# A second ending by tokens for the last half of a hybrid encoder layer, and large tiles at multiples of 512 bytes

## The chip, the cores and the metric

One core of a Trainium2 chip. The metric is the device time of one execution in microseconds (us), the median of three runs.

## The reference

One encoder layer over 512 tokens with 1024 features, in float32:

```
x = x + 1/2 * swiglu(rmsnorm(x), gate1, up1, down1)       # 1024 -> 2816 -> 1024
h = rmsnorm(x); P = h @ w_in                              # 1024 -> 3072
y = concat(rmsnorm(hyena(P[:, :1536])), rmsnorm(attention(P[:, 1536:])))
x = x + y @ w_out
x = x + 1/2 * swiglu(rmsnorm(x), gate2, up2, down2)
out = rmsnorm(x)            # x * rsqrt(mean(x*x) + 1e-6) * gain, per token
swiglu(h, g, u, d) = (silu(h @ g) * (h @ u)) @ d
```

Hyena is two long convolutions with gates, done through Fourier tables; the attention is a mixture of dilated windows. Neither is touched by the change.

## The kernel before

**Layout.** Features stand on partitions: `x` is eight tiles of 128 features x 512 tokens. Every large product is split in three (`mm3`, lines 144 to 148): each operand is a rounded high part and a low part, and high x high, high x low and low x high are added up in one PSUM bank. In a call the first operand is the one loaded into the array (a weight load, `PEld` in the profile), the second is streamed. In the FFNs and the projections weights are loaded and 512 tokens are streamed. Weights come in chunks of 128 x 1024, which ScalarE rounds (`wh`) and VectorE subtracts (`wl`).

**The FFN** (`ffn`, from line 319) runs twice over halves of the 22 hidden blocks: 11 times a gate and an up product of eight blocks each (`pgu`, streaming `xh`/`xl`), then the down product of the half, eight output blocks of 11 (`pd`, streaming `gh`/`gl`, the rounded and the low part of the hidden values). In the last half of the second FFN the output blocks 6 and 7 are done for one half of the tokens and then for the other: four groups of 33 matmuls with 256 columns. `tail` (line 1231) ends each: it adds the result to `x`, squares it, and sums over features with matmuls against `ones`. After block 7 it takes root and reciprocal, spreads the reciprocal over partitions with two matmuls against the identity (`spread`, line 312, tile `pb`), multiplies all eight blocks of `x` with it and sends them in four transfers of 256 KB, by turns on ScalarE's and SyncE's queue.

`done2` (line 1225) runs for blocks 0 to 5 when they are complete: their squares are added into `ssq` on GpSimd, and ScalarE multiplies them by the final gain.

**The order** of instructions on each engine is fixed while the program is built by a planner (`Merge`, line 71): streams of work ask for an engine with an estimated cost, and the one that can start first goes first, with a priority on ties.

**Where tiles stand.** A pool's tiles lie one behind the other in the order in which they are first asked for, each rounded up to 32 bytes. The main pool (`g.wp`, line 1110) starts at 16,512 bytes: `x` 16 KB, `cols` 352 bytes, `eps`, `ones` 512 bytes, `warm`, then raw and split weights, the identity, `xh`, `xl`, `ssq` and so on, and four small tiles for root and reciprocal at its end. The stages' pools stand behind it, those of side "right" at the upper end. So the large tiles start at these distances behind a multiple of 512: `x` 128, `ones` 0, all weight chunks, the identity, `xh`, `xl`, `ssq` 32, all of the stages' left pools (`z`, `u`, `gh`, `gl`, `yg`) 160, and the filter stage's tables and tiles (`ftab`, `fh`, `fl`) 480.

Of the kernel before, what the change touches and what calls it, by code (L numbers as in the profile page):

```python
# [35 lines left out]
NG1, NGM, NGH, NGA, NG2, NGF, NCW, NCB = 0, 8, 16, 20, 24, 32, 40, 76  # L36
NCOL = 88
WR, WB, HQ, SB, UC, ZB, X1B, UR = 2, 3, 3, 3, 3, 3, 3, 3
TWO_PI = 2.0 * math.pi


# [25 lines left out]
def wait(ev):  # L67
    return "W", ev
# [172 lines left out]
class SumSq:  # L241
# [38 lines left out]
    def rstd_cols(self, n, lag, res, m, ev):  # L280


        g, nc = self.g, self.g.nc
        yield on_v(0.0, lag)
        parts = self.sums()
        yield on_p(0.9 * len(parts), ps=1)
        pc = psum(g, "pc")
        for b in range(4):
            for i, t in enumerate(parts):
                nc.tensor.matmul(pc[:, b:b + 1], t[:, b * P:(b + 1) * P], g.ones[:, 0:1],  # L290
                                 start=i == 0, stop=i == len(parts) - 1)
        yield on_v(0.5, 0.4)
        std = g.wp.tile([P, 4], F32, tag="std", name="std", bufs=2)
        nc.scalar.activation(std, pc[:, 0:4], AF.Sqrt, bias=g.eps, scale=1.0 / n)
        rc = g.wp.tile([P, 4], F32, tag="rc", name="rc", bufs=2)
# [23 lines left out]
def ffn(g, m, fp, xg, nrm, nev, done, tail=None):  # L319
# [31 lines left out]
    for h in range(2):  # L351
        for f in range(HALF):
            pgu = []
            for _ in range(2):
                wc = g.w.take()
                ps = psum(g, "pgu")
                for k in range(DT):
                    if k == 3:
                        m.spawn(g.w.tick(), -1)
                    if k % 2 == 0:  # L360
                        yield on_p(1.3, 0.0, ps=int(k == 0))
                    mm3(nc, ps, wblk(wc, k), xg[k], k == 0, k == DT - 1)
                pgu.append(ps)
            ev = evs[h, f] = Event()
            m.spawn(evac(f, *pgu, ev), 0)
        wc, used = None, 8
        nd = DT - 2 if h == 1 and tail else DT
        for d in range(nd):
            ps = psum(g, "pd")
            for k in range(HALF):  # L370
                if used == 8:
                    wc, used = g.w.take(), 0
                if used == 3:
                    m.spawn(g.w.tick(), -1)
                if d == 0:
                    yield wait(evs[h, k])
                yield on_p(0.65, 0.0, ps=int(k == 0))
                mm3(nc, ps, wblk(wc, used), gt[k], k == 0, k == HALF - 1)
                used += 1
            m.spawn(devac(d, ps, h == 1), 0)  # L380
        if nd == DT:
            continue
        blk = []
        for th in range(2):
            for d in range(nd, DT):
                ps = psum(g, "pd")
                for k in range(HALF):
                    if th == 0:
                        if used == 8:
                            wc, used = g.w.take(), 0  # L390
                        if used == 3:
                            m.spawn(g.w.tick(), -1)
                        blk.append(wblk(wc, used))
                        used += 1
                    yield on_p(0.32, 0.0, ps=int(k == 0))
# [38 lines left out]
def filters(g, m, pool, tpool, a, start, done):  # L434
# [668 lines left out]
def body(ctx: ExitStack, tc: tile.TileContext, a: dict, out: bass.AP):  # L1103
# [19 lines left out]
    g.warm = warm = g.wp.tile([P, 1], F32, tag="warm", name="warm")  # L1123
    nc.scalar.activation(warm, g.eps, AF.Silu)
    ps = psum(g, "warm")
    for _ in range(NWARM):
# [5 lines left out]
        if d == 1:  # L1132
            g.w.start()
    g.w.load(1)
    g.ident = g.wp.tile([P, P], F32, tag="ident", name="ident")
    make_identity(nc, g.ident)


# [78 lines left out]

    with pool("f2", **over) as fp:
        ss3 = SumSq(g)
        n2, nev = {}, Event()  # L1220
        gain = lambda d: g.cols[:, NGF + d:NGF + d + 1]
        sq = {}
# [8 lines left out]
        def tail(d, th, ps):  # L1231

            hs = slice(th * CW, (th + 1) * CW)
            x = g.x[d][:, hs]
            if d == DT - 2:
                yield on_p(0.4, 0.0, ps=1)
                pc.append(psum(g, "pc"))
                for b in range(2):
                    bs = slice((2 * th + b) * P, (2 * th + b + 1) * P)
                    nc.tensor.matmul(pc[th][:, b:b + 1], ss3.acc[:, bs], g.ones[:, 0:1],  # L1240
                                     start=b == 0, stop=False)
            yield on_v(0.35)
            nc.vector.scalar_tensor_tensor(out=x, in0=ps[:, 0:CW], scalar=0.5, in1=x,
# [4 lines left out]
            nc.scalar.activation(sq[d][:, 0:CW], x, AF.Square)  # L1248
            yield on_p(0.3)
            for b in range(2):  # L1250
                nc.tensor.matmul(pc[th][:, b:b + 1], sq[d][:, b * P:(b + 1) * P],
                                 g.ones[:, 0:1], start=False, stop=d == DT - 1 and b == 1)
            if d < DT - 1:
                return
            yield on_v(0.3, 0.6)
            std = g.wp.tile([P, 4], F32, tag="std", name="std", bufs=2)
            nc.scalar.activation(std[:, 0:2], pc[th][:, 0:2], AF.Sqrt, bias=g.eps, scale=1.0 / D)
            rc = g.wp.tile([P, 4], F32, tag="rc", name="rc", bufs=2)
            nc.vector.reciprocal(rc[:, 0:2], std[:, 0:2])
            yield on_p(0.5, 0.2, ps=1)  # L1260
            pb = psum(g, "pb")
            for b in range(2):
                spread(g, pb[:, b * P:(b + 1) * P], rc[:, b:b + 1], P)
            for c in range(DT // 2):
                yield on_v(0.7)
                o = g.wp.tile([P, 2, CW], F32, tag="xh", name="o", bufs=DT)
                for i in range(2):
                    e = 2 * c + i
                    if e < DT - 2:
                        nc.vector.tensor_tensor(out=o[:, i], in0=g.x[e][:, hs], in1=pb[:, 0:CW], op=ALU.mult)  # L1270
                    else:
                        nc.vector.scalar_tensor_tensor(out=o[:, i], in0=g.x[e][:, hs], scalar=gain(e),
                                                       in1=pb[:, 0:CW], op0=ALU.mult, op1=ALU.mult)
                (nc.sync if c % 2 else nc.scalar).dma_start(
                    out[2 * c:2 * c + 2, :, hs].rearrange("d p s -> p d s"), o)
            m.free(ps=2)

        m.spawn(ffn(g, m, fp, at.x2, n2, nev, done2, tail), 1)

# [2 lines left out]
            yield from ss2.rstd(D, L2, n2, m, nev)  # L1282

        m.spawn(norm2(), 0)
        m.run()


# [58 lines left out]
def _layout(i):  # L1346
# [7 lines left out]
        k, m = w.shape  # L1354
        return w.reshape(k // P, P, m // P, P).transpose(2, 1, 0, 3)

    def down(w):
        b = w.reshape(2, HALF, P, DT, P).transpose(0, 3, 1, 2, 4)
        b = b.reshape(2 * DT * HALF // 8, 8, P, P)
        return b.transpose(0, 2, 1, 3).reshape(-1, P, 1024)  # L1360

    for f in ("1", "2"):
        o[f"w{f}g"] = stationary(n[f"ffn{f}_w_gate"]).reshape(FT, P, 1024)
        o[f"w{f}u"] = stationary(n[f"ffn{f}_w_up"]).reshape(FT, P, 1024)
        o[f"w{f}d"] = down(n[f"ffn{f}_w_down"])
# [11 lines left out]
    o["fw1"] = n["hy_filt_w1"]  # L1377
    o["fw23"] = np.concatenate([n["hy_filt_w2"], n["hy_filt_w3"], n["hy_filt_w3"]], axis=1)
    o["fwo"] = n["hy_filt_w_out"].reshape(FW, 2, 2, C).transpose(1, 2, 0, 3).reshape(2, P, C)
    o["skip"] = n["hy_filt_skip"].reshape(1, 2 * C)  # L1380
    return {k: np.ascontiguousarray(v) for k, v in o.items()}

# [17 lines left out]
```

## Time and profile before

| | us |
|---|---|
| median of 3 runs | 1048.6 (1047.63 to 1049.46) |
| the profiled execution | 1048.07 |
| its span, first to last instruction | 1046.3 |
| TensorE busy | 1032.0 (99%) |
| VectorE busy | 604.5 (58%) |
| ScalarE busy | 402.5 (38%) |
| mean granted TensorE clock | 0.995 of 2.4 GHz |

PE is TensorE's matmuls, PEld its weight loads, DVE VectorE, ACT ScalarE, POOL GpSimd, SP SyncE. A matmul's own duration includes its way through the array and overlaps the next one; the pace is read from start to start. A line such as L146 is a line of the kernel; L146 to L148 are the three products of `mm3`. A matmul of plain float32 operands appears as two instructions.

### The profile page before, as it was taken

What the parts mean: (1) busy time and instruction counts of PE and PEld (TensorE: products, weight loads), DVE (VectorE), ACT (ScalarE), POOL (GpSimd) and SP (SyncE); (2) the same over time, 40 slices, a digit from 0 to 9 for tenths busy, and PEclk for the clock granted to TensorE, in tenths of its full rate; (3) what the DMA queues carried; (4) which work ended last, traced back from release to release, by engine and by line L of the source; (5) the groups of instructions that cost most, each with busy time, mean ns of one, the idle gap of its engine ahead of it and who ended that gap; (6) DMA issues with size and microseconds to landing.
All of it is one profiled execution on the core that took longest, in us unless ns stands there. A gap on an engine that the chain in (4) does not pass through costs nothing.

```text
span 1046.3 us, 12667 instructions
## 1 busy us (share of the span) xinstructions
PE 1032.0 (99%) x5012; PEld 844.7 (81%) x5012; DVE 604.5 (58%) x834; ACT 402.5 (38%) x594; POOL 45.9 (4%) x37
## 2 busy tenths in 40 slices
PE   9999999999999999999998999999999999999997
PEld 7877888888888888888886778888888888888886
DVE  5676646554676444887999744764453235444332
ACT  6433432233334332344347874543232213333341
POOL 4000000000000111000000000210000000000010
PEclk9999999999999999999999999999999999999998
DMA  6333423533255222234435311233322332332222
GB/s 216 129 124 106 126 91 118 174 98 104 91 170 171 92 90 91 66 114 143 143 105 186 122 42 61 81 101 101 101 89 93 101 100 86 96 101 101 93 69 81
DMA packets 43513, 114.25 MB, mean 109 GB/s; under 512 B 5082, under 2 KB 12314, under 8 KB 43453
## 3 DMA queue, kind: packets, MB, share of 16 engines
q1 hardware_dynamic: 41644, 111.30, 33.3%
q10 hardware_dynamic: 1808, 2.14, 0.6%
q8 instruction: 39, 0.64, 0.3%
q14 instruction: 22, 0.17, 0.1%
HBM read 106.08 MB, written 7.34 MB: 108 GB/s over the span
## 4 chain that ended last, share of the span: by engine, by line
PE 96%; DVE 2%; ACT 1%; issue 1%; DMA 1%; SPq 0%; DVEq 0%; ACTq 0%
PE pgu L146 15%; PE pgu L147 15%; PE pgu L148 15%; PE pd L146 8%; PE pd L148 8%; PE pd L147 8%; PE pp L146 3%; PE pp L148 3%; PE pp L147 3%; PE pw L146 2%; PE pw L148 1%; PE pw L147 1%; PE po L1008 1%; PE ppt L996 1%; PE pqk L1039 1%; PE pv L146 1%
## 5 line engine op out<-in xcount | busy, mean ns | idle before, releaser
L188 ACT ACTIVATE wh<-wr 128x1024 fp32r<-128x1024 f32 x159 | 168.5, 1060 | 411.9 <-PE pgu L147 143.1
L146 PE MATMUL pgu<-xh,wh 128*128 128x512 f32 x704 | 275.4, 391 | 0.4 <-ACT wh L580 0.4
L147 PE MATMUL pgu<-xl,wh 128*128 128x512 f32 x704 | 274.4, 390 | 0.3 <-DVE xl L236 0.3
L148 PE MATMUL pgu<-xh,wl 128*128 128x512 f32 x704 | 274.5, 390 | 0.1
L194 DVE TENSOR_TENSOR wl<-wr,wh 128x1024 fp32r<-128x1024 f32 x159 | 198.1, 1246 | 114.3 <-ACT wh L188 110.0
L146 PEld LDWEIGHTS pgu<-xh,wh 128*128 128x128 f32 x704 | 132.2, 188 | 31.0 <-issue 2.9
L147 PEld LDWEIGHTS pgu<-xl,wh 128*128 128x128 f32 x704 | 132.1, 188 | 29.6 <-DVE xl L236 1.4
L148 PEld LDWEIGHTS pgu<-xh,wl 128*128 128x128 f32 x704 | 132.1, 188 | 28.3 <-DVE wl L581 0.4
L146 PE MATMUL pd<-gh,wh 128*128 128x512 f32 (+1 forms) x374 | 143.2, 383 | 0.0
L147 PE MATMUL pd<-gl,wh 128*128 128x512 f32 (+1 forms) x374 | 142.7, 382 | 0.0
L148 PE MATMUL pd<-gh,wl 128*128 128x512 f32 (+1 forms) x374 | 142.7, 382 | 0.0
L256 POOL TENSOR_TENSOR ssq<-ssq,sq 128x512 f32<-128x512 f32 x31 | 45.2, 1457 | 975.5 <-ACT sq L252 974.6
L331 DVE TENSOR_TENSOR u<-pgu,rb 128x512 f32<-128x512 f32 x44 | 30.3, 690 | 97.3 <-PE pgu L148 97.3
L147 PEld LDWEIGHTS pd<-gl,wh 128*128 128x128 f32 x374 | 70.3, 188 | 15.1
L148 PEld LDWEIGHTS pd<-gh,wl 128*128 128x128 f32 x374 | 70.3, 188 | 15.0
L146 PEld LDWEIGHTS pd<-gh,wh 128*128 128x128 f32 x374 | 70.3, 188 | 15.0
L329 DVE TENSOR_TENSOR z<-pgu,rb 128x512 f32<-128x512 f32 x44 | 30.4, 691 | 60.6 <-PE pgu L148 60.5
L146 PE MATMUL pp<-xh,wh 128*128 128x512 f32 x128 | 50.0, 391 | 0.0
L147 PE MATMUL pp<-xl,wh 128*128 128x512 f32 x128 | 49.9, 390 | 0.0
L148 PE MATMUL pp<-xh,wl 128*128 128x512 f32 x128 | 49.8, 389 | 0.0
L343 DVE SCALAR_TENSOR_TENSOR x<-pd,x 128x512 f32<-128x512 f32 x30 | 20.7, 690 | 42.7 <-PE pd L148 42.6
L336 ACT ACTIVATE gh<-u 128x512 fp32r<-128x512 f32 x44 | 27.7, 632 | 24.2 <-DVE u L333 23.8
(207 smaller groups left out, 1189.3 us busy)
## 6 DMA issues: line engine op xcount, KB each, us to landing
wr<-w1u SPq DMA_DIRECT2D x22, 512.0 KB, 3.4
wr<-w1d SPq DMA_DIRECT2D x22, 512.0 KB, 3.4
wr<-w2g SPq DMA_DIRECT2D x22, 512.0 KB, 3.4
wr<-w2u SPq DMA_DIRECT2D x22, 512.0 KB, 3.4
wr<-w2d SPq DMA_DIRECT2D x22, 512.0 KB, 3.4
wr<-w1g SPq DMA_DIRECT2D x21, 512.0 KB, 3.4
wr<-win SPq DMA_DIRECT2D x16, 512.0 KB, 3.4
pe<-negb SPq DMA_DIRECT2D x32, 256.0 KB, 3.2
```

The lines of the kernel that those rows point to most:

```text
L146: nc.tensor.matmul(ps, lh, rh, start=start, stop=False)
L147: nc.tensor.matmul(ps, lh, rl, start=False, stop=False)
L148: nc.tensor.matmul(ps, ll, rh, start=False, stop=stop)
L188: self.g.nc.scalar.activation(self.hi[i], self.raw[i], AF.Copy)
L194: self.g.nc.vector.tensor_tensor(out=self.lo[i], in0=self.raw[i], in1=self.hi[i].bitcast(F32), op=ALU.subtract)
L256: g.nc.gpsimd.tensor_tensor(out=self.acc, in0=self.acc, in1=sq, op=ALU.add)
L329: nc.vector.tensor_tensor(out=z, in0=pg, in1=rb, op=ALU.mult)
L331: nc.vector.tensor_tensor(out=u, in0=pu, in1=rb, op=ALU.mult)
L336: nc.scalar.activation(hi, u, AF.Copy)
L343: nc.vector.scalar_tensor_tensor(out=g.x[d], in0=ps, scalar=0.5, in1=g.x[d], op0=ALU.mult, op1=ALU.add)
L996: nc.tensor.transpose(ts[e][:, js], pes[e][:, js], g.ident)
L1008: nc.tensor.matmul(po[e * HD:(e + 1) * HD, b * P:(b + 1) * P], self.mx.v[j][:, h * HD:(h + 1) * HD], tt[e][:, j * P:(j + 1) * P], start=j ...
```

## The change

*The end.* In the last half of the second FFN the output blocks 6 and 7 are done together for the first 256 tokens (the two blocks by turns for each hidden block; the weights of the 22 pairs are laid out for it in memory), and `tail` ends these as before. For each of the two blocks of 128 tokens of the second half the operands are exchanged: the hidden values of 128 tokens are loaded into the array and 256 columns of weights are streamed, so that the result has tokens on partitions. For these tokens `turned` transposes all eight blocks of `x` on TensorE ahead (two PSUM banks each, held until the end), sums `ssq` over features into one column, and copies features 768 to 1023 to SBUF. `by_token` then adds, takes square and sum in one instruction, root and reciprocal as columns, multiplies, and sends rows of 512 features in two transfers. The gains of the last 256 features are loaded as a row, spread over partitions (`grow`). The output has another layout, undone on the host.

*The tiles.* Small tiles (`cols`, `eps`, `warm`, roots, reciprocals, the new columns) go to a pool of their own, `g.sp`, ahead of the main pool, with a filler of 224 bytes; a filler of 480 bytes stands in the pool of the tables. The identity is asked for behind `ones`. After that all large tiles start at multiples of 512 bytes.

```diff
 def ffn(...):            # last half, behind output blocks 0 to 5
-        blk = []
-        for th in range(2):
-            for d in range(nd, DT):
-                ps = psum(g, "pd")
-                for k in range(HALF):
...
-                    hs = slice(th * CW, (th + 1) * CW)
-                    mm3(nc, ps[:, 0:CW], blk[(d - nd) * HALF + k], (gt[k][0][:, hs], gt[k][1][:, hs]),
-                        k == 0, k == HALF - 1)
-                m.spawn(tail(d, th, ps), 0)
+        blk, ps = [], [psum(g, "pd") for _ in range(2)]
+        yield on_p(0.0, 0.0, ps=2)
+        for k in range(HALF):
...
+            if used == 2:
+                m.spawn(g.w.tick(), -1)
+            blk.append(wblk(wc, used // 2, CW))
+            for i in range(2):
+                yield on_p(0.35, 0.0)
+                mm3(nc, ps[i][:, 0:CW], wblk(wc, used + i), (gt[k][0][:, 0:CW], gt[k][1][:, 0:CW]),
+                    k == 0, k == HALF - 1)
+            used += 2
+        for i in range(2):
+            m.spawn(tail(nd + i, ps[i]), 0)
+        for b in (2, 3):
+            ps, bs = psum(g, "pd"), slice(b * P, (b + 1) * P)
+            for k in range(HALF):
+                yield on_p(0.35, 0.0, ps=int(k == 0))
+                mm3(nc, ps[:, 0:CW], (gt[k][0][:, bs], gt[k][1][:, bs]), blk[k], k == 0, k == HALF - 1)
+            m.spawn(tail(b, ps, True), -1)
 def filters(...):
     g.itab = split_tab(g, tpool, "itab", a["itab"])
+    tpool.tile([P, 120], F32, tag="fill", name="fillr")
 def body(...):
+    g.sp = ctx.enter_context(pool("sp"))
+    g.sp.tile([P, SMALL], F32, tag="fill", name="fill")
     g.wp = ctx.enter_context(pool("wp"))
...
-    g.cols = g.wp.tile([P, NCOL], F32, tag="cols", name="cols")
-    g.eps = g.wp.tile([P, 1], F32, tag="eps", name="eps")
+    g.cols = g.sp.tile([P, NCOL], F32, tag="cols", name="cols")
+    g.eps = g.sp.tile([P, 1], F32, tag="eps", name="eps")
...
+    g.ident = g.wp.tile([P, P], F32, tag="ident", name="ident")
+    g.warm = warm = g.sp.tile([P, 1], F32, tag="warm", name="warm")
...
+        g.grow = fp.tile([P, CW], F32, tag="grow", name="grow")
+        nc.scalar.dma_start(g.grow, a["grow"])
         def done2(d):
...
+            if d == DT - 3:
+                m.fire(xev)
+        def turned():
+            yield wait(xev)
+            for b in (2, 3):
+                bs = slice(b * P, (b + 1) * P)
+                yield on_p(1.1, ps=3)
+                held[b] = pa, pr = psum(g, "pta"), psum(g, "ptr")
+                for e in range(DT):
+                    nc.tensor.transpose((pa, pr)[e // 4][:, e % 4 * P:(e % 4 + 1) * P], g.x[e][:, bs], g.ident)
+                ps = psum(g, "pc")
+                nc.tensor.matmul(ps[:, 0:1], ss3.acc[:, bs], g.ones[:, 0:1], start=True, stop=True)
+                yield on_v(0.2, 0.5)
+                pre[b] = g.sp.tile([P, 1], F32, tag=f"pre{b}", name="pre")
+                nc.vector.tensor_scalar(out=pre[b], in0=ps[:, 0:1], scalar1=1.0 / D, scalar2=EPS,
+                                        op0=ALU.mult, op1=ALU.add)
+                m.free(ps=1)
+                xr = fp.tile([P, S], F32, tag="z", name="xr", bufs=2)
+                nc.scalar.copy(xr[:, 0:CW], pr[:, CW:S])
+                held[b] += (xr[:, 0:CW],)
+        def by_token(b, ps):
+            pa, pr, xr = held[b]
+            yield on_v(0.45)
+            y = fp.tile([P, S], F32, tag="u", name="y", bufs=2)
+            nc.vector.scalar_tensor_tensor(out=y[:, 0:CW], in0=ps[:, 0:CW], scalar=0.5, in1=xr,
+                                           op0=ALU.mult, op1=ALU.add)
+            m.free(ps=1)
+            yield on_a(0.6)
+            sa = g.sp.tile([P, 1], F32, tag=f"sa{b}", name="sa")
+            nc.scalar.activation(xr, y[:, 0:CW], AF.Square, accum_out=sa)
+            nc.vector.tensor_tensor(out=y[:, CW:S], in0=y[:, 0:CW], in1=g.grow, op=ALU.mult)
+            std = g.sp.tile([P, 4], F32, tag="std", name="std", bufs=2)
+            nc.scalar.activation(std[:, 0:1], sa, AF.Sqrt, bias=pre[b], scale=1.0 / D)
+            yield on_v(0.9, 0.2)
+            rc = g.sp.tile([P, 4], F32, tag="rc", name="rc", bufs=2)
+            nc.vector.reciprocal(rc[:, 0:1], std[:, 0:1])
+            o = [g.wp.tile([P, S], F32, tag="xh", name="o", bufs=DT) for _ in range(2)]
+            nc.scalar.activation(o[0], pa, AF.Copy, scale=rc[:, 0:1])
+            nc.vector.tensor_scalar_mul(o[1][:, CW:S], y[:, CW:S], rc[:, 0:1])
+            nc.vector.tensor_scalar_mul(o[1][:, 0:CW], pr[:, 0:CW], rc[:, 0:1])
+            m.free(ps=2)
+            dst = out[1].rearrange("(t c) -> t c", c=D)[(b - 2) * P:(b - 1) * P]
+            nc.scalar.dma_start(dst[:, 0:S], o[0])
+            nc.sync.dma_start(dst[:, S:D], o[1])
...
+        m.spawn(turned(), 0)
```

## Rows read from the trace of the kernel before

**Rows 1.** The page: busy time, clock in 40 slices, the chain that ended last.

```profile
PE 1032.0 (99%) x5012; PEld 844.7 (81%) x5012; DVE 604.5 (58%) x834; ACT 402.5 (38%) x594; POOL 45.9 (4%) x37
...
PEclk9999999999999999999999999999999999999998
...
PE 96%; DVE 2%; ACT 1%; issue 1%; DMA 1%; SPq 0%; DVEq 0%; ACTq 0%
```

**Rows 2.** Timeline, TensorE: start (us), duration (us), what, at the ends of runs.

```profile
653.78 0.39 PE L147 MATMUL pw<-yg,wh 128*128 128x512 f32 x1
...
670.27 0.39 PE L146 MATMUL pgu<-xh,wh 128*128 128x512 f32 x1
...
790.91 0.40 PE L146 MATMUL pd<-gh,wh 128*128 128x512 f32 x1
...
852.51 0.39 PE L146 MATMUL pgu<-xh,wh 128*128 128x512 f32 x1
...
972.20 0.40 PE L146 MATMUL pd<-gh,wh 128*128 128x512 f32 x1
...
1018.39 0.28 PE L146 MATMUL pd<-gh,wh 128*128 128x256 f32 x1
...
1021.95 0.28 PE L146 MATMUL pd<-gh,wh 128*128 128x256 f32 x1
```

**Rows 3.** Chain that ended last, in order of time: start, length (us), what.

```profile
692.25 0.86 PE pb L270 x2
```

**Rows 4.** Timeline, TensorE, filter stage: split products at offset 480.

```profile
298.94 0.39 PE L146 MATMUL pf<-fh,ftabh 128*128 128x512 f32 x1
299.17 0.40 PE L147 MATMUL pf<-fl,ftabh 128*128 128x512 f32 x1
299.40 0.39 PE L148 MATMUL pf<-fh,ftabl 128*128 128x512 f32 x1
299.63 0.39 PE L146 MATMUL pgu<-xh,wh 128*128 128x512 f32 x1
```

**Rows 5.** Groups of VectorE: what, count, busy us, mean ns, idle before.

```profile
L331 DVE TENSOR_TENSOR u<-pgu,rb 128x512 f32<-128x512 f32 x44 | 30.3, 690 | 97.3 <-PE pgu L148 97.3
L343 DVE SCALAR_TENSOR_TENSOR x<-pd,x 128x512 f32<-128x512 f32 x30 | 20.7, 690 | 42.7 <-PE pd L148 42.6
```

**Rows 6.** Timeline of the end, from the last down matmul on.

```profile
1036.85 0.28 PE L148 MATMUL pd<-gh,wl 128*128 128x256 f32 x1
1037.16 0.42 DVE L1243 SCALAR_TENSOR_TENSOR x<-pd,x 128x256 f32<-128x256 f32 x1 [2.69 <-PE pd L148]
1037.68 0.42 ACT L1248 ACTIVATE sq<-x 128x256 f32<-128x256 f32 x1 [4.14 <-DVE x L1243]
...
1038.15 0.61 PE L1251 MATMUL pc<-ones,sq 128*128 128x1 f32 x4 [1.03 <-ACT sq L1248]
1038.80 0.26 ACT L1257 ACTIVATE std<-pc,eps 128x2 f32<-128x2 f32 x1 [0.70 <-PE pc L1251]
1039.09 0.17 DVE L1259 RECIPROCAL rc<-std 128x2 f32<-128x2 f32 x1 [1.50 <-ACT std L1257]
...
1039.31 0.71 PE L312 MATMUL pb<-ident,rc 128*128 128x128 f32 x4 [0.55 <-DVE rc L1259]
1040.06 2.08 DVE L1270 TENSOR_TENSOR o<-x,pb 128x256 f32<-128x256 f32 x6 [0.80 <-PE pb L312]
...
1042.05 0.87 DVE L1272 SCALAR_TENSOR_TENSOR o<-x,cols,pb 128x256 f32<-128x256 f32 x2
```

**Rows 7.** DMA from 1025 to 1047 us, GB/s in 40 slices.

```profile
GB/s 0 0 0 0 0 0 0 30 0 0 0 0 0 0 147 339 343 255 337 345 142 0 0 0 0 0 0 0 0 0 175 337 339 339 345 341 32 0 0 0
```

**Rows 8.** Chain and timeline: transposes; the end of ssq; column sums.

```profile
613.56 0.87 PE ppt L996 x8
...
1020.69 1.28 POOL L256 TENSOR_TENSOR ssq<-ssq,sq 128x512 f32<-128x512 f32 x1 [5.86 <-ACT sq L252]
...
1032.15 0.50 PE L1240 MATMUL pc<-ones,ssq 128*128 128x1 f32 x4
```

More of the change, by code (lines that the diff above doesn't have):

```diff
@@ L382, in ffn @@
             continue
-        blk = []
-        for th in range(2):
-            for d in range(nd, DT):
-                ps = psum(g, "pd")
-                for k in range(HALF):
[L388 to L395, printed above, removed]
-                    hs = slice(th * CW, (th + 1) * CW)
-                    mm3(nc, ps[:, 0:CW], blk[(d - nd) * HALF + k], (gt[k][0][:, hs], gt[k][1][:, hs]),
-                        k == 0, k == HALF - 1)
-                m.spawn(tail(d, th, ps), 0)
+        blk, ps = [], [psum(g, "pd") for _ in range(2)]
+        yield on_p(0.0, 0.0, ps=2)
+        for k in range(HALF):
+            if used == 8:
+                wc, used = g.w.take(), 0
+            if used == 2:
[14 more added lines that the diff above has]
+            m.spawn(tail(b, ps, True), -1)
 def split_tab(g, pool, name, src):
@@ new lines, in by_token @@
+        def by_token(b, ps):
[9 more added lines that the diff above has]
+            nc.vector.tensor_tensor(out=y[:, CW:S], in0=y[:, 0:CW], in1=g.grow, op=ALU.mult)
+            std = g.sp.tile([P, 4], F32, tag="std", name="std", bufs=2)
+            nc.scalar.activation(std[:, 0:1], sa, AF.Sqrt, bias=pre[b], scale=1.0 / D)
+            yield on_v(0.9, 0.2)
+            rc = g.sp.tile([P, 4], F32, tag="rc", name="rc", bufs=2)
+            nc.vector.reciprocal(rc[:, 0:1], std[:, 0:1])
[7 more added lines that the diff above has]
+            nc.sync.dma_start(dst[:, S:D], o[1])
@@ L1234, in tail @@
+        def tail(d, ps, turn=False):
+            if turn:
+                yield from by_token(d, ps)
+                return
+            hs = slice(0, CW)
             x = g.x[d][:, hs]
@@ L1238, in tail @@
                 for b in range(2):
-                    bs = slice((2 * th + b) * P, (2 * th + b + 1) * P)
-                    nc.tensor.matmul(pc[th][:, b:b + 1], ss3.acc[:, bs], g.ones[:, 0:1],
+                    nc.tensor.matmul(pc[0][:, b:b + 1], ss3.acc[:, b * P:(b + 1) * P], g.ones[:, 0:1],
                                      start=b == 0, stop=False)
@@ L1250, in tail @@
             for b in range(2):
-                nc.tensor.matmul(pc[th][:, b:b + 1], sq[d][:, b * P:(b + 1) * P],
+                nc.tensor.matmul(pc[0][:, b:b + 1], sq[d][:, b * P:(b + 1) * P],
                                  g.ones[:, 0:1], start=False, stop=d == DT - 1 and b == 1)
@@ L1255, in tail @@
             yield on_v(0.3, 0.6)
-            std = g.wp.tile([P, 4], F32, tag="std", name="std", bufs=2)
-            nc.scalar.activation(std[:, 0:2], pc[th][:, 0:2], AF.Sqrt, bias=g.eps, scale=1.0 / D)
-            rc = g.wp.tile([P, 4], F32, tag="rc", name="rc", bufs=2)
+            std = g.sp.tile([P, 4], F32, tag="std", name="std", bufs=2)
+            nc.scalar.activation(std[:, 0:2], pc[0][:, 0:2], AF.Sqrt, bias=g.eps, scale=1.0 / D)
+            rc = g.sp.tile([P, 4], F32, tag="rc", name="rc", bufs=2)
             nc.vector.reciprocal(rc[:, 0:2], std[:, 0:2])
+            m.free(ps=1)
             yield on_p(0.5, 0.2, ps=1)
@@ L1274, in tail @@
                 (nc.sync if c % 2 else nc.scalar).dma_start(
-                    out[2 * c:2 * c + 2, :, hs].rearrange("d p s -> p d s"), o)
-            m.free(ps=2)
+                    out[0].rearrange("(d p s) -> p d s", p=P, s=CW)[:, 2 * c:2 * c + 2], o)
+            m.free(ps=1)
         m.spawn(ffn(g, m, fp, at.x2, n2, nev, done2, tail), 1)
@@ L1355, in stationary, with down @@
         return w.reshape(k // P, P, m // P, P).transpose(2, 1, 0, 3)
-    def down(w):
+    def down(w, turn):
         b = w.reshape(2, HALF, P, DT, P).transpose(0, 3, 1, 2, 4)
+        b = b.reshape(2 * DT * HALF, P, P).copy()
+        if turn:
+            b[-2 * HALF:] = b[-2 * HALF:].reshape(2, HALF, P, P).transpose(1, 0, 2, 3).reshape(-1, P, P)
         b = b.reshape(2 * DT * HALF // 8, 8, P, P)
@@ L1364, in _layout @@
         o[f"w{f}u"] = stationary(n[f"ffn{f}_w_up"]).reshape(FT, P, 1024)
-        o[f"w{f}d"] = down(n[f"ffn{f}_w_down"])
+        o[f"w{f}d"] = down(n[f"ffn{f}_w_down"], f == "2")
     o["win"] = stationary(n["w_in"][:, :5 * C]).reshape(20, P, 1024)
@@ L1379, in _layout @@
     o["fwo"] = n["hy_filt_w_out"].reshape(FW, 2, 2, C).transpose(1, 2, 0, 3).reshape(2, P, C)
+    o["grow"] = np.broadcast_to(n["final_norm_g"][-CW:], (P, CW))
     o["skip"] = n["hy_filt_skip"].reshape(1, 2 * C)
@@ L1391 @@
            for k, v in arrays.items()}
-    out = nc.dram_tensor("out", (DT, P, S), F32, kind="ExternalOutput").ap()
+    out = nc.dram_tensor("out", (2, CW * D), F32, kind="ExternalOutput").ap()
     with tile.TileContext(nc) as tc:
@@ L1395 @@
     r = run_bass_kernel_spmd(nc, [arrays], core_ids=[0])
-    got = np.asarray(r.results[0]["out"]).reshape(D, S).T
+    got = np.asarray(r.results[0]["out"])
+    got = np.concatenate([got[0].reshape(D, CW).T, got[1].reshape(CW, D)])
     y = np.empty((1, S, D), np.float32)
```

8 lines of the change are left out of this document (2 added, 6 removed).

## The prediction

> **What bounds the kernel now.** I read the page first [rows 1]: TensorE is busy 99% of the span, the chain that ended last is TensorE for 96%, and its clock is at full speed (2.4 GHz) from end to end. So two things can move the time: the pace of the matmuls, and what follows the last one. Everything else (weight splits, evictions, loads) lies beside TensorE.
>
> The pace comes from the timeline, by counting matmuls between two starts [rows 2]. Between 852.51 and 972.20 us stand the 528 gate and up matmuls of one half (11 blocks x 2 x 8 x 3): 119.69 us, so 226.7 ns each. Between 790.91 and 852.51 stand 264 down matmuls: 233.3 ns. From 972.20 to 1018.39 stand 198: 233.3 ns again. The output projection has 71 in 16.49 us: 232.3 ns. All have 512 columns, which at 2.4 GHz are 213.3 ns; so 13.4 ns are over in the first kind and 20.0 in the second. In the last stage 30 matmuls of 256 columns take 1018.39 to 1021.95, 118.7 ns each, 12.0 over their 106.7. Nobody is waited for in these stretches, and the pace holds however busy the other engines are; it belongs to the operands.
>
> What differs between the paces is where the streamed operand starts. By the addresses told above, xh and xl start 32 bytes past a multiple of 512, gh, gl and yg 160 bytes; the weights are at 32 in all of these. Nothing else separates gate and up from down: same shape, same three products, same weight buffers.
>
> **Part one, large tiles at multiples of 512 bytes.** No arithmetic changes; the small tiles go to a pool of their own, two fillers are added, and every large tile then starts at a multiple of 512. It touches all of the roughly 4,000 matmuls that split a product in three, and no matmul of before has both operands there, so the new pace must be bounded.
>
> *Bound below.* One product of before loads its array from `ones` (offset 0) and shows what a stream without this loss can do: 0.86 us for 512 columns [rows 3]. At 2.4 GHz that is 4.02 cycles a column, so some 4 ns over for a whole number of cycles. It asks for a new element far less often than the split matmuls, so it is a floor, not an estimate: about 2 ns over 213.3, or 215.5 ns.
>
> *Bound above.* The pf matmuls of the filter stage have both operands at 480, 32 bytes before a multiple of 512. Three take 298.94 to 299.63 us, 230 ns each, beside gate and up matmuls at 227 [rows 4]. A common offset is thus no promise, and 233.3, the worst steady pace seen, is the other end.
>
> *The value I take.* The nearest row is that of gate and up: operands at equal offsets, 32 bytes from the boundary. The three points rank by distance to the boundary (32: 226.7; 32 on the other side: 230; 160: 233.3), so at distance zero I take no worse than 226.7, and, as no row shows better, exactly that. Then:
> - gate and up (2112) and the mixer's projections at offset 32: nothing;
> - down, 990 with 512 columns: 990 x 6.6 ns = 6.5 us off;
> - the last 132 with 256 columns: their excess shrinks as 13.4 to 20.0, so 12.0 becomes 8.0 ns: 0.5 us off;
> - output projection, 192: 192 x 5.6 = 1.1, of which I count 1.0 as parts of it wait for others.
>
> Sum 8.0 us off.
>
> VectorE and ScalarE: the eviction of a 512-column bank takes 690 ns whether its SBUF operand lies at 160 (u) or at 128 (x) [rows 5]; I count nothing, and TensorE covers them anyway.
>
> A rule of the Trainium skill speaks against this part: the page "SBUF — State Buffer", section "Specifications (TRN2)", has lines of 16 bytes whose crossing costs. All tiles of before start at multiples of 32, hence on a line, so by that rule nothing would change; but it doesn't give the 6.6 ns between offsets 32 and 160 either, which the rows show.
>
> **Part two, the end.** *Now:* from the start of the last down matmul at 1036.85 to the span's end at 1046.28 are 9.43 us [rows 6]. In it stand, one after the other: addition 1037.16, square, column sums on TensorE (0.61), root, reciprocal, spreading on TensorE (0.71), eight vector products from 1040.06 to 1042.92, then 3.36 us of issue, landing and closing.
>
> *After:* the last block has tokens on partitions, so the sum over its 256 features comes with the square (`accum_out`), the reciprocal is already a column, and both TensorE steps and six of eight products leave the path. With the same durations and hand-overs: addition to 1037.58, square 1037.68 to 1038.10, root to 1038.40, reciprocal to 1038.60, two products of 256 (0.42 each; ScalarE's 0.7 for its 512 runs beside) to 1039.47, then the same 3.36. Both halves are now sent at once instead of one by one: 256 KB more in flight at some 340 GB/s [rows 7] is 0.8 us. End at 1043.6: 2.7 us off.
>
> *Added on TensorE:* 16 transposes, eight of which take 0.87 us [rows 8], so 1.74, and two column sums of 0.25; away go one pair of column sums over ssq (0.50 at 1032.15) and one over sq (the same form): 1.0. Net 1.24 us, all on the path. They wait for x5 and for ssq, with the matmuls of the last stage queued behind them. In before ssq is complete at 1021.97 [rows 8], the last of them, 3.6 us after the last stage begins; by the planner's costs (0.7, 0.7 and 1.0 behind block 5, perhaps a tick of 1.15) they stand 2.5 to 3.7 us behind that point. I count 0 of at most 0.6 us.
>
> *Moved:* the first half of the tokens now ends both blocks together, so its whole ending (2 additions, 8 products, four 256 KB transfers) lies beside the 66 matmuls of the turned blocks, 7.8 us. VectorE there has some 4.5 us for it and 1.7 us for each turned block, 7.9 us in all: full. The turned endings have precedence, so one pair of products (0.84 us) may stand ahead of the last reciprocal: 0 to 0.9, I take 0.3. ScalarE's and SyncE's queues hold output transfers that wait for VectorE; what stands behind them on ScalarE is later work of the same planner, so no new wait. 1.57 MB must leave before the last 512 KB, 4.6 us at 340 GB/s, and there is time for it. The row of gains (`grow`, 128 KB) is loaded at the opening of the stage, some 350 us ahead of its use. The interleaved order takes weight chunks earlier by one tick; the last chunk was split by 1019.3, 10 us ahead.
>
> Sum of part two: -2.7 + 1.24 + 0.3 = -1.2 us, bounds -1.5 and 0.
>
> **Rivals.** *B, full pace:* the whole excess comes from starts off the boundary, and all split matmuls go to about 215.5 ns. For it: the excess grows with the distance. Against it: no steady row below 226. Time: gate and up 2112 x 11.2 = 23.7, projections 576 x 11.2 = 6.5, down 990 x 17.8 = 17.6, output 192 x 16.8 = 3.2, the last stage 132 x 10 = 1.3: 52, of which I count 50, and 1.2 of the end: 997.4. It may also come in part.
> The Trainium skill gives B a pace: "TensorE: Matmul & The Clock Gate", section "Back-to-back issue gap", has N/2.4 + 2.5 ns, 215.8 for 512 columns; no run here shows it for these operands.
>
> *C, nothing:* the pace hangs on the distance between the two operands or on something I haven't seen, and evens out; only the end counts: 1047.4.
>
> *D, slower:* weight load and stream, which start together, meet in the same places when all starts are alike, as pf's 230 hints. If gate, up and the projections at 32 (2688) go to the 233.3 of down: 2688 x 6.6 = 17.7 us, less 1.2: 1065. Over all 3,870 split matmuls with 512 columns the mean of before is 228.7 ns; should all take one pace, the 1.2 us of the end are used up and the kernel is slower from 229.0 ns on, so 2.3 ns lost in the fast kind are enough. Against it: gate and up, also alike, are the fastest kind.
>
> **How the numbers follow.** The profiled execution took 1048.07 us for a span of 1046.3, within the three runs around 1048.6; I subtract from the median: 1048.6 - 8.0 - 1.2 = 1039.4. Chances: forecast A 0.40, B (in full or part) 0.28, C 0.14, D 0.18. A alone spans 1036 to 1043. The range must take in B and C, and leaves D out: 994 to 1050. A measurement of this kernel can tell about 0.2%, 2.1 us; C lies within it, so faster 0.68, same 0.14, slower 0.18.
>
> **What would show it.** The starts of gate and up, of down and of the output projection in the timeline of after: all at 227 ns for A, all near 216 for B, unchanged for C, 230 and more for D. At the end: 6.7 us instead of 9.4 from the last matmul, and transposes in one piece without a wait ahead of them. It would be wrong if a third offset decides, or if the last products queue behind the first half's.

## The result, and the profile after

The changed kernel takes 1036.84 us (median of four, 1036.45 to 1037.98) beside 1048.87 (1047.63 to 1049.46) for the kernel before: 0.9889 of its time, interval 0.9874 to 0.9904, some 12 us less. The forecast was 1039.4. The profiled execution, the longest of the four, took 1037.98 us for a span of 1036.2; between the two profiled spans lie 10.1 us. Its mean granted clock was 0.996, that of the other three 0.998. The stretch at half the clock that it holds (shown below) is worth some 1.5 us; whether the other three had one isn't on record.

The page of after, as [rows 1]:

```profile
PE 1023.6 (99%) x5016; PEld 844.6 (82%) x5016; DVE 604.7 (58%) x835; ACT 404.8 (39%) x601; POOL 45.1 (4%) x37
...
PEclk9999999999999999999999999999999999999999
...
PE 96%; DVE 2%; issue 1%; ACT 1%; DMA 0%; DVEq 0%; SPq 0%; ACTq 0%
```

TensorE still bounds everything, with the clock as before and four instructions more. So the gain is in its pace. The timeline of after, TensorE, at the ends of the same stretches as [rows 2] (start, duration, what):

```profile
602.35 0.47 PE L147 MATMUL pw<-yg,wh 128*128 128x512 f32 x1
...
665.39 0.39 PE L147 MATMUL pgu<-xh,wh 128*128 128x512 f32 x1
...
785.98 0.39 PE L147 MATMUL pd<-gh,wh 128*128 128x512 f32 x1
...
845.82 0.39 PE L147 MATMUL pgu<-xh,wh 128*128 128x512 f32 x1
...
965.50 0.39 PE L147 MATMUL pd<-gh,wh 128*128 128x512 f32 x1
...
1010.38 0.28 PE L147 MATMUL pd<-gh,wh 128*128 128x256 f32 x1
...
1013.97 0.28 PE L147 MATMUL pd<-gh,wh 128*128 128x256 f32 x1
```

Down: 264 matmuls from 785.98 to 845.82, 226.7 ns each, and 198 from 965.50 to 1010.38, 226.7 again (before 233.3). Gate and up: 528 in 119.68 us, 226.7, unchanged. The last 256-column products: 30 in 3.59 us, 119.7 ns; before 118.7.

The end of after, timeline, as [rows 6], with the first transpose of each turned block ahead:

```profile
1014.33 0.60 PE L1257 MATMUL pta<-ident,x 128*128 128x128 f32 x4
...
1016.86 0.60 PE L1257 MATMUL pta<-ident,x 128*128 128x128 f32 x4
...
1030.03 0.28 PE L149 MATMUL pd<-wh,gl 128*128 128x256 f32 x1
1030.35 0.42 DVE L1274 SCALAR_TENSOR_TENSOR y<-pd,xr 128x256 f32<-128x256 f32 x1 [0.90 <-PE pd L149]
1030.81 0.42 ACT L1279 ACTIVATE xr<-y 128x256 f32<-128x256 f32 x1 [1.42 <-DVE y L1274]
...
1031.88 0.69 ACT L1287 ACTIVATE o<-pta,rc 128x512 f32<-128x512 f32 x1 [0.23 <-DVE rc L1285]
...
1032.15 0.48 DVE L1289 TENSOR_SCALAR o<-ptr,rc 128x256 f32<-128x256 f32 x1
```

From the last down matmul at 1030.03 to the span's end at 1036.18 are 6.15 us (before 9.43). Between addition and products stands no TensorE step any more, and the transposes have no wait ahead of them. The DMA rate of after from 1015 to 1037 us, as [rows 7]:

```profile
GB/s 0 0 0 0 0 0 0 0 0 30 0 0 0 0 0 0 0 0 0 0 0 274 380 300 205 272 197 320 413 406 93 0 0 156 413 380 4 0 0 0
```

The last rows of 2 KB go out at 380 to 413 GB/s; before, pieces of 1 KB went at some 340. Not all of that is the length of the rows: the kernel with the new tiles and the old end (e2, below) sends pieces of 1 KB at 350 to 384 at its end, from 1017 to 1039 us:

```profile
GB/s 0 0 0 0 0 0 0 0 0 30 0 0 0 0 0 0 307 384 263 317 300 337 0 0 0 0 0 0 0 0 0 0 326 384 380 350 374 93 0 0
```

Stage by stage, from the starts of each kind of matmul in the two timelines (us; the first column is before):

| stretch | before | after | difference |
|---|---|---|---|
| start and first gate and up block | 137.22 | 136.94 | -0.28 |
| four down blocks (the first with filter work) | 238.81 | 232.11 | -6.70 |
| second gate and up block (filter work beside) | 132.45 | 131.71 | -0.74 |
| mixer | 205.89 | 206.31 | +0.42 |
| output projection | 63.69 | 63.04 | -0.65 |
| gate and up of the second FFN | 240.33 | 240.27 | -0.06 |
| from the first 256-column product to the end | 27.89 | 25.80 | -2.09 |
| span | 1046.28 | 1036.18 | -10.10 |

In both profiles the mixer holds a stretch of 3.4 us in which TensorE's granted clock is 0.5, so 1.2 GHz in place of 2.4. The two stretches of before below (limits; length and busy time of PE, PEld, DVE, ACT, POOL; granted clock; DMA share and GB/s) show it, and ahead of it a TensorE that is busy for 1.44 of 3.4 us, as it waits for ScalarE. The third line is the mixer of e3, the new end with the old tiles, whose profile has no such stretch:

```profile
568.90:572.30 3.40, 1.44 (x11) 0.95 (x10) 3.40 (x9) 2.35 (x7) 0.00 (x0) 1.00 0.42 153
572.40:575.70 3.30, 3.30 (x14) 2.43 (x15) 3.30 (x8) 2.90 (x8) 0.00 (x0) 0.50 0.00 1
...
401.40:605.77 204.37, 199.85 (x1201) 165.43 (x1200) 173.24 (x291) 105.75 (x197) 5.58 (x4) 1.00 0.38 121
```

The mixer takes 204.4 and 204.7 us in the profiles without such a stretch (e3, e6), 205.8 to 206.4 with one, and 207.6 and 208.0 with twice its length (e1, e7). So such a stretch is worth some 1.5 us, and the +0.42 in the row of the mixer lies within the 0.6 by which profiles with one of them differ.

### The profile page after: what moved, and what is told of

Its sections match the earlier page's. It is cut to its first block, busy times and chain, and to the rows that moved or that the text cites. A ratio compares the mean times of both kernels' runs of the same rounds, so it can differ in the third digit from the quotient of the medians.

```text
span 1036.2 us, 12682 instructions
## 1 busy us (share of the span) xinstructions
PE 1023.6 (99%) x5016; PEld 844.6 (82%) x5016; DVE 604.7 (58%) x835; ACT 404.8 (39%) x601; POOL 45.1 (4%) x37
## 4 chain that ended last, share of the span: by engine, by line
PE 96%; DVE 2%; issue 1%; ACT 1%; DMA 0%; DVEq 0%; SPq 0%; ACTq 0%
PE pgu L148 15%; PE pgu L149 15%; PE pgu L147 15%; PE pd L147 8%; PE pd L149 8%; PE pd L148 8%; PE pp L147 3%; PE pp L148 3%; PE pp L149 3%; PE pw L147 2%; PE pw L148 1%; PE pw L149 1%; PE po L1016 1%; PE ppt L1004 1%; PE pqk L1047 1%; PE pv L149 1%
## 5 line engine op out<-in xcount | busy, mean ns | idle before, releaser
L147 PE MATMUL pd<-gh,wh 128*128 128x512 f32 (+1 forms) x352 | 134.8, 383 | 0.0
L149 PE MATMUL pd<-gh,wl 128*128 128x512 f32 (+1 forms) x352 | 134.6, 382 | 0.0
L148 PE MATMUL pd<-gl,wh 128*128 128x512 f32 (+1 forms) x352 | 134.6, 382 | 0.0
L148 PEld LDWEIGHTS pd<-gl,wh 128*128 128x128 f32 x352 | 66.2, 188 | 12.9
L147 PEld LDWEIGHTS pd<-gh,wh 128*128 128x128 f32 x352 | 66.1, 188 | 12.9
L149 PEld LDWEIGHTS pd<-gh,wl 128*128 128x128 f32 x352 | 66.1, 188 | 12.9
```

Source lines behind the costliest of these rows:

```text
L147: nc.tensor.matmul(ps, lh, rh, start=start, stop=False)
L148: nc.tensor.matmul(ps, lh, rl, start=False, stop=False)
L149: nc.tensor.matmul(ps, ll, rh, start=False, stop=stop)
```

## The experiments

Two theories stood against each other. **N**: the pace goes by how far the starts of the operands lie from a multiple of 512 bytes, as the prediction had it. **R**: it goes by the difference between the start of the streamed operand and the start of the loaded one, wherever they are.

**e1_probe: the disputed cost by itself.** Groups of 30 like matmuls stand ahead of the first stage of the changed kernel, each with one stream offset (s), one load offset (w), one size.

```diff
...
+        for mo, so, n, mc in PROBES:
+            ps = psum(g, f"q{n}x{mc}s{mo}w{so}z")
+            for i in range(30):
+                nc.tensor.matmul(ps[0:mc, 0:n], qw[:, so // 4:so // 4 + mc], qm[:, mo // 4:mo // 4 + n],
+                                 start=i == 0, stop=i == 29)
```

> The kernel after, with groups of 30 equal split-type matmuls ahead of its first stage, each group with its own start (in bytes behind a multiple of 512) of the streamed and of the loaded operand; the extra groups are not used for the output. Theory N (the pace depends on how far the streamed operand starts from a multiple of 512): with the loaded operand at 0 and 512 columns, 227 ns at 0, 16, 32 and 480, rising to 233 at 160 and 256; equal offsets of 160 and 256 also 233. Theory R (only the distance between the two starts counts): 227 ns at all equal offsets (32, 64, 128, 160, 256, 480), and 230 to 233 where they differ by 96 to 256. Both: 227 at 0 and 0. Neither expects less than 226. With a load of 64 or 32 columns instead of 128: 227 if the streaming alone makes the excess, nearer to 216 if the load takes turns with it. 256 columns: 120 ns at 0 and 0.

The timeline of the probe, TensorE: the eighth and the 28th matmul of a group, each merged with the one behind it (x2), so 20 paces lie between the two starts. The tile's name tells the columns streamed, the columns loaded, and the two offsets.

```profile
45.72 0.63 PE L1163 MATMUL q512x128s128w0z<-qm,qw 128*128 128x512 f32 x2
50.38 0.63 PE L1163 MATMUL q512x128s128w0z<-qm,qw 128*128 128x512 f32 x2
66.72 0.61 PE L1163 MATMUL q512x128s256w0z<-qm,qw 128*128 128x512 f32 x2
71.25 0.62 PE L1163 MATMUL q512x128s256w0z<-qm,qw 128*128 128x512 f32 x2
163.65 0.62 PE L1163 MATMUL q512x128s160w160z<-qm,qw 128*128 128x512 f32 x2
168.19 0.62 PE L1163 MATMUL q512x128s160w160z<-qm,qw 128*128 128x512 f32 x2
177.34 0.61 PE L1163 MATMUL q512x128s480w480z<-qm,qw 128*128 128x512 f32 x2
181.87 0.62 PE L1163 MATMUL q512x128s480w480z<-qm,qw 128*128 128x512 f32 x2
227.84 0.63 PE L1163 MATMUL q512x64s0w0z<-qm,qw 128*64 128x512 f32 x2
232.44 0.63 PE L1163 MATMUL q512x64s0w0z<-qm,qw 128*64 128x512 f32 x2
```

Stream at 128 with load at 0: 4.66 us for 20, 233 ns. Both at 160, or both at 480: 4.54 and 4.53, 227 ns. Stream at 256 with load at 0: 227 too. So does every group with equal starts (32, 64, 128, 160, 256, 480) and 0 against 256 in either direction; the other differences gave 229 to 234.5. N falls: 480 and 160 are as good as 32. R holds so far, with the difference taken modulo 256. A load of 64 columns in place of 128 doesn't help (230 ns). With 256 columns it is the other way: 120.0 ns at equal starts, 118.7 with stream at 160 and load at 32.

**e2_tiles_only and e3_end_only: each part alone.** The first puts the tiles of the kernel before as the change does; the second has the new end with the tiles where they were.

```diff
 e2: the kernel before, with
+SMALL = 88
...
+    g.sp = ctx.enter_context(pool("sp"))
+    g.sp.tile([P, SMALL], F32, tag="fill", name="fill")
...
+    tpool.tile([P, 120], F32, tag="fill", name="fillr")
 e3: the kernel after, with
-    g.sp = ctx.enter_context(pool("sp"))
-    tpool.tile([P, 120], F32, tag="fill", name="fillr")
...
```

> The kernel before with the large tiles at multiples of 512 and the old end. Forecast A: 8 us less than before, so 1040 to 1041, down matmuls at 226.7 ns. If the new end were the larger part: 1046 or more.

> The kernel before with the new end and all large tiles where they were (weights, xh, xl 32, gh, gl 160, tables 480). By the working of the prediction 1.2 us less than before (0 to 1.5), 1047 to 1048, down matmuls still 233.3 ns. Together with the tiles alone it should add up to the change: 12 us less.

e2: 1039.94 us, ratio 0.9918 (0.9906 to 0.9931), some 8.5 us less than before. e3: 1045.75, ratio 0.9979 (0.9970 to 0.9988), some 2.3 less. Together 11, beside about 12 for the change: the parts add up. The timeline of e2 at the ends of the last 198 down products of 512 columns, and its last down matmul:

```profile
966.32 0.39 PE L147 MATMUL pd<-gh,wh 128*128 128x512 f32 x1
...
1011.20 0.28 PE L147 MATMUL pd<-gh,wh 128*128 128x256 f32 x1
...
1029.76 0.28 PE L149 MATMUL pd<-gh,wl 128*128 128x256 f32 x1
```

44.88 us, 226.7 ns, with the old end; from 1029.76 to the end of its span at 1038.91 are 9.15. The same places in e3:

```profile
971.42 0.40 PE L147 MATMUL pd<-gh,wh 128*128 128x512 f32 x1
...
1017.62 0.28 PE L147 MATMUL pd<-gh,wh 128*128 128x256 f32 x1
...
1037.13 0.28 PE L149 MATMUL pd<-wh,gl 128*128 128x256 f32 x1
```

46.20 us, 233.3 ns, and 6.20 from 1037.13 to 1043.33. Its last stage is 19.51 us long, before 18.46: the turned end adds 1.05 us on TensorE without any change of tiles.

**e4_left_32: equal starts, none at a multiple of 512.** One filler in the kernel before moves the stages' left pools from 160 to 32, where the weights stand.

```diff
+        g.wp.tile([P, 96], F32, tag="fill", name="fill")
         ss3 = SumSq(g)
```

> The kernel before with a filler of 384 bytes that moves the stages' tiles alone: gh, gl, yg from 160 to 32, where the weights are; nothing stands at a multiple of 512. Theory R and theory N: down at 226.7 to 227 ns, output projection too, 7 to 8 us less than before, 1041. If multiples of 512 themselves are what counts: down stays at 233, 1048.6.

1041.77 us, ratio 0.9938 (0.9925 to 0.9952), 6.5 us less than before. The timeline of e4, the ends of the first down block of the second FFN:

```profile
788.22 0.39 PE L146 MATMUL pd<-gh,wh 128*128 128x512 f32 x1
...
848.06 0.39 PE L146 MATMUL pgu<-xh,wh 128*128 128x512 f32 x1
```

59.84 us, 226.7 ns: one filler is enough for the down products. It stays 1.8 us above e2; e8 will show where 1.3 of them lie.

**e6_left_160 and e7_stage_128: R against N inside the kernel.** In e6 all left tiles of the changed kernel stand at 160, weights and streams alike. In e7 the weights stay at 0 and the stages' pools go to 128.

```diff
 e6
-SMALL = 56
+SMALL = 96
 e7
+        g.wp.tile([P, 32], F32, tag="fill", name="fill2")
         ss3 = SumSq(g)
```

> The kernel after with 160 bytes more in the first filler: all large tiles of the left pools (weights, xh, xl, gh, gl, yg, x) start at 160, none at a multiple of 512. Theory R (only the difference counts): gate, up, down and output projection at 226.7 ns as in the kernel after, and its time, 1036.8 within 2 us (the mixer's tables stay at 0, so its 256-column products differ by 160 from them and the filter's don't). Theory N (distance to the boundary): 233 for all of them, 1036.8 + 3,870 x 6.6 ns = 1062.

> The kernel after with 128 bytes more at the end of the main pool: the stages' tiles (gh, gl, yg, z, u) start at 128, the weights stay at 0. Theory R: down back at 233.3 ns and the output projection at 232.5, 990 x 6.6 + 192 x 5.6 = 7.6 us more, less some 0.2 us as 256 columns run at 118.7: 1044.2. Theory N: 990 x 6 ns as well (128 from the boundary), so this run sizes the effect in the new kernel and doesn't separate the two.

e6: 1040.14, ratio 0.9920 (0.9903 to 0.9936). e7: 1045.64, ratio 0.9971 (0.9958 to 0.9983). The down block in the timeline of e6, and then of e7:

```profile
787.23 0.39 PE L147 MATMUL pd<-gh,wh 128*128 128x512 f32 x1
...
847.07 0.39 PE L147 MATMUL pgu<-xh,wh 128*128 128x512 f32 x1
```

```profile
792.68 0.40 PE L147 MATMUL pd<-gh,wh 128*128 128x512 f32 x1
...
854.27 0.39 PE L147 MATMUL pgu<-xh,wh 128*128 128x512 f32 x1
```

59.84 us with both at 160, 61.59 with 128 against 0: R on both sides. In e7 the four down blocks and the output projection lose 6.50 and 0.72 us against after, 7.2 of the 8.8 between the medians. But e6 is 3.3 us above after, more than the 2 that R allowed. In its profile 1.8 of it lie in the first down block and the second gate and up block, beside the filter's work, and there the right pool (at 0) met left tiles at 160. Another 1.1 lie ahead of it, in the start and the first gate and up block. The mixer of this profile is 1.65 us shorter, as it has no stretch at half the clock.

**e8_no_right_filler and e9_stage_256.** e8 is the changed kernel without the filler in the pool of the tables, so that right tiles stand at 480 and left ones at 0; e9 is e8 with the stages' left pools at 256.

```diff
 e8
-    tpool.tile([P, 120], F32, tag="fill", name="fillr")
 e9, besides
+        g.wp.tile([P, 64], F32, tag="fill", name="fill2")
         ss3 = SumSq(g)
```

> After without the filler of 480 bytes in the pool of the tables: the filter stage's tables and tiles and the mixer's right tiles stand at 480 again, everything on the left at 0. By the theory that the pace goes by the difference of the two starts, the filter's own products stay alike (both at 480: 226.7 ns), and only the products between a right and a left tile change: 96 of 512 columns go to 231 to 233 (0.5 us lost) and 192 of 256 columns go back from 119.5 to 117.5 to 118.8 ns (0.2 to 0.4 us regained); so the filler is worth nearly nothing: 0 to 0.5 us over the changed kernel, 1036.8 to 1037.4. By the theory that what counts is the distance to a multiple of 512, the filter's products go back to 230 and more, and the time is 1 to 2 us over the changed kernel, 1038 to 1039.

> As the run without the filler of 480 bytes, and the stages' left pools (hidden values, normed heads) stand at 256 while the weights stay at 0. If the pace goes by the difference of the two starts modulo 256, the 990 down products of 512 columns and the output projection stay at 226.7 ns, those of 256 columns at 120.0 ns, and the time is that of the run without the filler, within 0.5 us. If equal offsets modulo 512 are needed, down and output projection go to 230 to 233.3: 1182 products by 3.3 to 6.6 ns, 3.9 to 7.8 us more.

e8: 1041.0 us, ratio 0.9921 (0.9906 to 0.9936), so some 3.4 us more than the change's ratio gives. R had 0 to 0.5; N, with 1 to 2, came nearer in time, but for a reason that doesn't hold. Where the time goes stands in the timeline of e8, a triple of filter products (`pf`, both operands at 480) among gate and up (both at 0):

```profile
242.50 0.39 PE L147 MATMUL pf<-fh,ftabh 128*128 128x512 f32 x1
...
243.20 0.39 PE L147 MATMUL pgu<-xh,wh 128*128 128x512 f32 x1
...
244.59 0.40 PE L147 MATMUL pgu<-xh,wh 128*128 128x512 f32 x1
...
246.65 0.39 PE L147 MATMUL pgu<-xh,wh 128*128 128x512 f32 x1
```

and at the like place of after, where all stand at 0:

```profile
240.78 0.39 PE L147 MATMUL pf<-fh,ftabh 128*128 128x512 f32 x1
...
241.46 0.39 PE L147 MATMUL pgu<-xh,wh 128*128 128x512 f32 x1
...
242.82 0.39 PE L147 MATMUL pgu<-xh,wh 128*128 128x512 f32 x1
...
244.86 0.39 PE L147 MATMUL pgu<-xh,wh 128*128 128x512 f32 x1
```

In after the triple and the six and nine matmuls behind it all take 227 ns (0.68, 1.36, 2.04 us). In e8 the triple takes 233 each (0.70 us), the six behind it 231.7 (1.39), and the next nine 228.9 (2.06), although each of them alone has equal starts. So R isn't whole: **a change of the common start costs too**, on the changing products and on ten or more behind them, until the pace has settled. The probe shows the same: in e1 the group with both operands at 64 stands behind the one with both at 32, and its first paces are 230, 224, 231, 235, 229, 232 and 231 ns before it keeps 227. The second gate and up block, same work in every kernel, measures it: 131.7 us where left and right stand alike (after, e2, e7), 132.5 with 32 beside 480 (before, e3, e4), 132.7 with 160 beside 0 (e6), 133.0 with 0 beside 480 (e8, e9). With the first down block, where filter products stand as well, e8 loses 1.96 us against after. The rest of the 3.4 is within the intervals. The same sum gives 1.3 of the 1.8 us between e4 and e2.

e9: 1041.51, ratio 0.9923 (0.9904 to 0.9942), that of e8. Timeline of e9, the same down block, `gh` at 256 and `wh` at 0:

```profile
788.79 0.39 PE L147 MATMUL pd<-gh,wh 128*128 128x512 f32 x1
...
848.63 0.39 PE L147 MATMUL pgu<-xh,wh 128*128 128x512 f32 x1
```

59.84 us: 256 is as good as 0, in the kernel as in the probe.

**e5_probe_fine: steps of 16 bytes, and which load counts.** As e1, with the load at 0 and the stream at 0, 16, ... 240; then two groups whose starts go by turns between 0 and 128. In `qown` each matmul's stream and own weights start alike, so that the load which runs beside it, the next one's, is 128 away; in `qnext` it is the reverse.

```diff
...
+          + [("qownz", 512, [(0, 0), (128, 128)], 0), ("qnextz", 512, [(0, 128), (128, 0)], 0),
...
```

> The kernel after with groups of 30 matmuls ahead of its first stage; the extra groups are not used for the output. By the first groups the pace hangs on the difference d of the two starts modulo 256 alone. So for 512 columns over d = 0, 16, ... 240: 226.7 ns at 0 alone, 229 at 64, 231.7 at 16, 232 to 235 elsewhere. For 256 columns, where 120.0 was seen at 0 and 118.7 at 128: 118 to 120 everywhere. Two crossed groups tell which load counts: in the first each matmul streams from where its own weights start (0 with 0, 128 with 128, by turns), but runs beside the load of the next one's, 128 away; in the second it is the other way round. If the load that runs beside the stream decides: 233 in the first, 226.7 in the second; if its own weights decide: the reverse. bfloat16 operands at d = 0 and 128: if the excess comes from reading 4 bytes a column, 216 for both; if from the weights' exchange, 227 too.

The timeline of this probe, eighth and 28th matmul, as for e1:

```profile
179.26 0.64 PE L1169 MATMUL qownz<-qm,qw 128*128 128x512 f32 x2
183.99 0.63 PE L1169 MATMUL qownz<-qm,qw 128*128 128x512 f32 x2
186.31 0.62 PE L1169 MATMUL qnextz<-qm,qw 128*128 128x512 f32 x2
190.91 0.62 PE L1169 MATMUL qnextz<-qm,qw 128*128 128x512 f32 x2
```

236.5 and 230 ns. The load that runs beside the stream matters more than the matmul's own; but neither group comes to the plain 233 or 227, so a rule for mixed starts stays open. In steps of 16 the difference 0 gave 226.7 ns, 16 already 231.7, and 240 (16 short of 256) 226.65; all others lay between 230.8 and 234.7. With 256 columns it is otherwise: 120.0 at 0, which none exceeds (80 takes as long), and 114.7 to 119 at most others, where 118 to 120 were expected. The 114.7, at 112, is no steady pace: thirteen matmuls at 113.3 stand between others of 116 to 121.

In bfloat16 the paces are 224 to 225 ns with a few up to 232, at a difference of 0 and of 128 alike: no price of the start is seen there. How much a bfloat16 matmul has over its columns can't be read, as the granted clock of this whole run was 0.95 (e1's probes had 1.00), at which 512 columns alone take 225 ns:

```profile
100.00:200.00 100.00, 99.95 (x668) 88.53 (x668) 0.00 (x0) 0.00 (x0) 0.00 (x0) 0.95 0.00 1
```

That clock shows something more. The fp32r paces (fp32r is the type of the split operands) are those of e1 all the same, 226.65 at 0, 231.65 at 16, 120.0 with 256 columns, and in the kernel behind the probes the four down blocks take 232.11 us and gate and up of the second FFN 240.28, as in after. Were 13.3 ns added to the columns' 225, it would be 238. So by these rows the 226.7 ns are a limit beside the columns, which didn't follow the clock from 1.00 to 0.95.

## Why the prediction came out

**Down products: right in size, for a wrong reason.** 6.5 us were foreseen, the four blocks give 6.7; that the number came out is luck. The step that failed is the ranking of three offsets by their distance to the boundary. It took the 230 ns of the filter triples [rows 4] for the steady pace at 480. Steady, 480 with 480 is 227 (e1); the triples are slow because they stand among products with another start: at 480 among products at 0 they take 233 (e8), and with all at 0, 227 (after). And down was slow at 160 not for the 160, but because its weights were at 32 (e6 against e7). The value taken, that of gate and up, was right because their two operands already stood alike. The prediction put the difference between gate and up and down on the start of the stream alone, though it had noted that the weights stood at 32 in both; what differed was the distance to them.

**Gate and up:** nothing foreseen, 240.33 to 240.27 us in the second FFN. **Output projection:** 1.0 foreseen, 0.65 measured.

**Last 256-column products: wrong sign.** 0.5 us off was foreseen by scaling the excess of the 512-column products; measured are 118.7 and 119.7 ns, 132 x 1.0 ns = 0.13 us more. Equal starts are the slow case here (e1, e5). For the mixer's 192 products of 256 columns the same holds, a mean of 117.6 before and 119.4 now, some 0.3 us that the prediction hadn't counted.

**The clock.** The prediction read full speed from end to end in [rows 1]. The 40 slices are too coarse for the 3.4 us at half the clock in the mixer. That didn't touch its sum, as both profiles have them, but it blurs every comparison of whole times by some 1.5 us.

**Not foreseen: the filter's neighbours.** 0.74 us of the second gate and up block, and of the first down block what it gained beyond the others (1.88 beside 1.75), come with right and left tiles at one start, by the 480-byte filler, which the prediction counted at nothing. It about makes up for the misses: by the profiles 6.7 + 0.74 + 0.65 - 0.13 - 0.3 = 7.7 us for the tiles, by the runs of e2 8.5 (7.2 to 9.9 by its interval), for the 8.0 forecast.

**The end: right in its steps, low in size.** Forecast 1.2 us less, measured alone 2.3 (e3). By its terms: TensorE's additions 1.24, measured 1.05 to 1.06 (19.65 us from the first 256-column product to the last in after, 18.46 before, 0.13 of it pace). From the last matmul to the end of the products 2.62, measured 2.60 (1030.03 to 1032.63). From there to the end 3.36 + 0.8 for sending both halves together; measured 3.55. That is the mis-sized term, 0.6 us: only 0.19 are added. The faster rate explains less than 0.2 of it (256 KB take 0.63 us at 413 GB/s). In before the output moves without a break in [rows 7], so its last 256 KB had to wait behind the earlier ones, and the 3.36 us held that wait; in after nothing moves for two slices (1.1 us) ahead of the last 512 KB. How much of the 0.6 each is worth wasn't measured. The 0.3 us for queuing behind the first half's products weren't there: those end at 1028.60, ahead of the last matmul.

**The rivals.** B (full pace, 215.5 ns): no split product of 512 columns in any group keeps below 226.6. At equal starts 13.3 ns more than the columns take at 2.4 GHz remain, with 256, 384 (173.35 ns in e1) and 512 columns alike. C (nothing but the end): out by e2; but one of its premises, that the pace hangs on the distance between the two operands, is what held, and not A's. D (slower where all starts are alike): out for equal starts; its idea, that load and stream hinder each other, fits `qown` and `qnext` (e5), but with 512 columns they do so least where their starts are equal modulo 256. What the prediction named as making it wrong, that another offset decides, is so for its reason and not for its time.

## What to carry to other kernels

For streams of fp32r matmuls with 512 columns and a weight load each, let the streamed and the loaded operand start at the same place modulo 256 bytes, and let products that stand among each other share that start; one filler did most of it (e4). Count such gains by kind of matmul: the shape with 256 columns went the other way. An odd pace in a short run of three between other work says nothing of the steady pace; look for a long run, or make one.

## What the runs showed of the hardware

- The pace of fp32r matmuls with 512 columns and a load of 128 each depends on where stream and load start relative to each other: 226.7 ns at a difference of 0 or 240 modulo 256, 229 to 237 at all others tried. Equal starts at 32, 64, 128, 160, 256 and 480 are as good as 0.
- The pace has a memory: after three products with another start, ten or more take 229 to 232 ns before 226.7 comes back (e8), though nothing of their own has changed. One difference, 64, was 228.9 in e1 and 233.3 in e5, so the difference alone doesn't fix the pace everywhere.
- At a granted clock of 0.95 the fp32r products of 512 columns kept 226.65 ns (e5), and the down blocks took 232.11 us as at 1.00. The 3.4 us at 0.5 in the mixer cost some 1.5 us.
- The load beside the stream isn't free. The Trainium skill says on its page "TensorE: Matmul & The Clock Gate", section "Step-by-step: what each phase is for", that loading the next weights takes no read bandwidth from the running matmul, over a port of its own; `qown` and `qnext`, which differ only in which load runs beside which stream, took 236.5 and 230 ns. So the load does act on the stream here, and the measurement decides against that part of the page; whether it is the reading at which they meet isn't shown. The same section lets the load's time go by its columns. The records agree (188 ns for 128 columns, 134 for 64, 108 for 32 in e1), but the pace with 64 columns was no better (230 against 227).

Not settled: why 256, why 240 is as good as 0 where 16 isn't, and why 256 columns prefer unequal starts. A version with a difference of 112 for the 256-column products wasn't tried. By e5 it would give at most 132 x 5.3 ns = 0.7 us at the end (an estimate from an unsteady pace), and it would bring in changes of start, which e8 shows to cost.
